# SSD chunks: the state product in three fp32r products of high and low halves

## The chip, the core and the metric

The kernel runs on one core of one Trainium2 chip. The metric is the time of one execution of the whole program on the device, in microseconds (us). Lower is better. All inputs lie in HBM when it starts, and all outputs are in HBM when it ends.

## The reference

The program is one inference step of a small two-layer encoder trunk on two groups of frames that share the weights: 1024 new frames ("prompt") and 32 frames of a running stream ("sample"). Layer one is a Mamba-2 SSD mixer, layer two an HGRN2 mixer; each is followed by a SwiGLU feed-forward part. The change touches only the SSD scan, which works in chunks of frames:

```python
def step(S, inp):
    xc, dtc, Bc, Cc = inp
    cum = jnp.cumsum(dtc * Ag, axis=1)
    ...
    xdt = xc * dtc[..., None]
    cb = jnp.einsum('btgn,bsgn->btsg', Cc, Bc)
    y = jnp.einsum('btsg,btsgh,bsghp->btghp', cb, decay, xdt)
    y = y + jnp.einsum('btgn,bghpn->btghp', Cc, S) * jnp.exp(cum)[..., None]
    last = cum[:, -1]
    w_end = jnp.exp(last[:, None] - cum)
    S = jnp.exp(last)[..., None, None] * S + jnp.einsum('bsgh,bsghp,bsgn->bghpn', w_end, xdt, Bc)
    return S, y
```

The last `einsum` is the state product: over the frames of a chunk, B (128 state entries) times the weighted x (8 heads of 64 entries, 512 in all). It is added to the decayed state S. Everything is float32.

## The kernel before

**Halves and phases.** The 1056 frames are worked in two halves: h = 0 has 512 prompt frames, h = 1 the other 512 and the 32 sample frames. The SSD layer runs first (to about 835 us), then its feed-forward part, then the HGRN2 layer and its own. Activations lie transposed, with features on the partitions and frames along the free axis.

**Large products.** Weights and activations are each split into a high half, rounded to fp32r by a copy on ScalarE, and a low half, the remainder, made by a subtraction on VectorE (`split` and `wsplit`). A product then is three TensorE matmuls per 128 rows, high x high, high x low and low x high, accumulated in PSUM: lines L316, L317 and L318 in `product`. Their outputs are called mm. Most of TensorE's time goes there.

**The SSD chunks.** For each half and each of 4 groups g (8 heads) the kernel walks over chunks of 128 frames: 4 in half 0, 4 and the one of 32 sample frames in half 1. That makes 16 + 20 = 36 calls of `ssd_chunk`, 32 of them with 128 frames and 4 with 32. A chunk takes the score product of B and C (L540), transposes x (L545), forms `xdt` and `xw` on VectorE (two ways of weighting x), builds the decay matrices `dec` on ScalarE (Relu with a bias for each of 8 heads, then Exp) and VectorE, transposes B (L561), copies it to `Btok` on ScalarE, multiplies the old state with C (L568), makes the state product (L571: B as weights 128 x 128, `xw` as the moving 512 columns, both fp32), adds it to S on VectorE, and computes the eight heads' outputs (L582). Each of these eight matmuls has weights of only 64 columns, and even and odd heads go to the lower and upper 64 output partitions. The helper lines L98 (`act`, ScalarE), L101 (`tt`, VectorE) and L104 (`stt`, VectorE) stand for all calls of these helpers, so one goes by tile names there: `fixed<-sc` on ScalarE is the copy to `Btok`, `yh<-Y` and `yl<-Y,yh` are a split elsewhere.

**Order.** A scheduler lays out each engine's instructions ahead of time: from the code's order, from a few priorities and from the times at which it believes operands ready, it picks the next instruction of each engine. Each engine then works its list strictly in order, and waits on semaphores where an operand is late. Between the steps of a chunk, TensorE is given large products (outputs mm) of other work: output projections, gate projections and the convolution inputs of the next group. So what a chunk's instructions follow on TensorE is chosen by the scheduler, and it can put a large product, or another step of the chunk, between any two matmuls.

**PSUM.** Five banks (mm) serve the large products, three (sc) rotate among all small results of the chunks.

Of the kernel before, what the change touches and what calls it, by code (L numbers as in the profile page):

```python
# [8 lines left out]
F32 = mybir.dt.float32  # L9
F32R = mybir.dt.float32r  # L10
U32 = mybir.dt.uint32
AF = mybir.ActivationFunctionType
# [4 lines left out]
P = 128  # L17
# [23 lines left out]

TW = 552
FIXED = 14368
BUFS = {"x": 12, "ys": 8, "cb": 4, "xd": 2, "de": 2, "ec": 2, "ss": 1, "xr": 2, "n": 4, "w": 3}
WIDTH = {k: TW for k in BUFS}


@with_exitstack
def trunk_kernel(ctx, tc, x_prompt, x_sample, state_ssd, cache_conv, state_hgrn,
# [5 lines left out]
    V, A, G, PE = nc.vector, nc.scalar, nc.gpsimd, nc.tensor  # L55

    cp = ctx.enter_context(tc.tile_pool(name="cp", bufs=1))
    tp = ctx.enter_context(tc.tile_pool(name="tp", bufs=1))
# [7 lines left out]
    def nm(s):  # L66
        uid[0] += 1
        return f"{s}_{uid[0]}"

    def T(tag, s, dt=F32):  # L70
        return tp.tile([P, WIDTH[tag]], dt, tag=tag, bufs=BUFS[tag], name=nm(s))

    def slot(tag, s):
        return T(tag, s, F32R) if isinstance(tag, str) else tag

    rings = {"diag": (0, 2), "cbm": (2, 2), "Btok": (4, 2), "hT": (0, 2), "hSp": (2, 4), "fss": (4, 2), "nco": (0, 1)}
    at = {}

    def small(s, w=P):

        at[s] = at.get(s, -1) + 1
        if s == "hec":
            return hec[at[s] % 3][:, :w]
        first, n = rings[s]
        return smalls[first + at[s] % n][:, :w]
# [11 lines left out]
    def act(out, in_, f, **kw):  # L97
        A.activation(out=out, in_=in_, func=f, **kw)  # L98

    def tt(out, a, b, op, eng=None):  # L100
        (eng or V).tensor_tensor(out=out, in0=a, in1=b, op=op)  # L101
# [23 lines left out]
    MUL, ADD, SUB = ALU.mult, ALU.add, ALU.subtract  # L125
# [5 lines left out]
    def place(w):  # L131
        used[0] += -(-w // 16) * 16
        return fixed[:, used[0] - -(-w // 16) * 16:][:, :w]
# [33 lines left out]
    xr = place(9)  # L167
# [362 lines left out]
    @lifted("chunk")  # L530
    def ssd_chunk(h, g, c, S, loads, u):
        o, n, smp = CHUNKS[h][c]
        Bt, Ct, xs, Y = u["x"][0], u["x"][1], u["x"][2:], u["Y"]
        cols, elast = dts[h]
        xo = o + (3 if smp else 0)
        Bx, Cx = Bt[:, xo:xo + n], Ct[:, xo:xo + n]
        h0 = g * 8
        cums, ec = loads
        ps = psum_sc()
        PE.matmul(ps[:n, :n], Bx, Cx, start=True, stop=True)  # L540
        cbm = small("cbm")
        tt(cbm[:n, :n], ps[:n, :n], cmask[:n, :n], MUL)
        ps = psum_sc()
        for j in range(4):
            PE.transpose(ps[:n, j * P:(j + 1) * P], xs[j][:, xo:xo + n], ident)  # L545
        x3 = ps[:n, :].rearrange("p (h q) -> p h q", q=64)
        xdt, xw = T("xd", "xdt")[:, :512], T("xd", "xw")[:, :512]
        tt(xdt[:n, :].rearrange("p (h q) -> p h q", q=64), x3,
           cols[:n, c, h0:h0 + 8].unsqueeze(2).to_broadcast([n, 8, 64]), MUL)
        tt(xw[:n, :].rearrange("p (h q) -> p h q", q=64), x3,  # L550
           cols[:n, c, 64 + h0:64 + h0 + 8].unsqueeze(2).to_broadcast([n, 8, 64]), MUL)
        for q in range(2):
            cb3 = T("de", "dec")[:, :512].rearrange("p (h t) -> p h t", t=P)
            for i in range(4):
                hh = 32 + h0 + 4 * q + i
                act(cb3[:n, i, :n], cums[q][:n, i, :n], AF.Relu, scale=-1.0, bias=cols[:n, c, hh:hh + 1])
            cums[q] = cb3
            act(cb3[:n, :, :n], cb3[:n, :, :n], AF.Exp, scale=-1.0)
            tt(cb3[:n, :, :n], cb3[:n, :, :n], cbm[:n, :n].unsqueeze(1).to_broadcast([n, 4, n]), MUL)
        ps = psum_sc()  # L560
        PE.transpose(ps[:n, :P], Bx, ident)  # L561
        Btok = small("Btok")
        act(Btok[:n, :], ps[:n, :P], AF.Copy)
        if ec is not None:
            y2 = psum_sc()
            y23 = y2.rearrange("p (j t) -> p j t", t=P)
            for j in range(4):
                PE.matmul(y23[:, j, :n], S[:, j * P:(j + 1) * P], Cx, start=True, stop=True)  # L568
            tt(ec[:, :, :n], y23[:, :, :n], ec[:, :, :n], MUL)
        pp = psum_sc()  # L570
        PE.matmul(pp, Btok[:n, :], xw[:n, :], start=True, stop=True)  # L571
        if ec is None:
            V.tensor_copy(S, pp)
        else:
            S3 = S.rearrange("p (h q) -> p h q", q=64)
            tt(S3, S3, elast[:, h0:h0 + 8, c:c + 1].to_broadcast([P, 8, 64]), MUL)
            tt(S, S, pp, ADD)
        y1 = psum_sc()
        y13 = y1.rearrange("p (j t) -> p j t", t=P)
        for i in range(8):  # L580
            r = 64 * (i % 2)
            PE.matmul(y13[r:r + 64, i // 2, :n], xdt[:n, i * 64:(i + 1) * 64], cums[i // 4][:n, i % 4, :n],  # L582
                      start=True, stop=True)
        yo = Y[:, :, o:o + n]
        if ec is None:
            act(yo, y13[:, :, :n], AF.Copy)
        else:
            tt(yo, y13[:, :, :n], ec[:, :, :n], ADD)
# [720 lines left out]
    for s, dst in ((0, conv_p), (1, conv_s)):  # L1309
        ps = psum_sc()  # L1310
# [41 lines left out]
```

## Time and profile before

| | us |
|---|---|
| Median of 3 runs | 2867.1 |
| Fastest and slowest of them | 2866.38, 2867.78 |
| Span of the profiled execution | 2867.3 |
| TensorE busy in it | 2838.4 (99%) |
| VectorE busy | 2131.5 (74%) |
| ScalarE busy | 1560.3 (54%) |
| Matmuls in it | 19704 |

How to read it: the span runs from the first to the last instruction of one profiled execution. An fp32 matmul shows as two records in a trace, an fp32r matmul as one, and so the 36 state products show as 72. The busy time of a matmul record includes its way through the array, in which the next one already streams. What a matmul costs in a stream is therefore read from the chain of waits, which gives each instruction the time from the end of its predecessor to its own end, or from the distance of starts. The columns of a window's row are, in this order, TensorE, its weight loads, VectorE, ScalarE and GpSimd, each with its busy us and number of instructions, then the granted clock (1.00 is full), the busy share of the DMA engines, and GB/s.

### The profile page before, as it was taken

How to read it: one execution, taken by the hardware profiler on the slowest of the kernel's cores; microseconds unless marked ns; L12 is line 12 of the kernel's file. 1: busy time of each engine (PE TensorE's matmuls, PEld its weight loads, DVE VectorE, ACT ScalarE, POOL GpSimd, SP SyncE). 2: the span in 40 equal slices, each digit the busy share in tenths (PEclk: the TensorE clock that was granted, in tenths of full speed). 3: DMA queues.
4: the chain of work that ended last, by engine and by line, in shares of the span. 5: the costliest groups of instructions: out<-in, count | busy, mean ns of one | idle time of the engine just before them, and what ended most of it. 6: DMA issues, size and time to landing. Idle time of an engine off the chain costs nothing.

```text
span 2867.3 us, 48953 instructions
## 1 busy us (share of the span) xinstructions
PE 2838.4 (99%) x19704; PEld 2614.7 (91%) x19704; DVE 2131.5 (74%) x3686; ACT 1560.3 (54%) x2910; POOL 44.1 (2%) x156
## 2 busy tenths in 40 slices
PE   8999999999999999999999999999999999999998
PEld 8778788999979999999999887899988999999998
DVE  7787887787787877797777556655568877787776
ACT  6665654564644644465444656555564644455544
POOL 1000000000100000000000000000000000000000
PEclk9999999999999999999999999999999999999999
DMA  6444334444322332333323222222222432333332
GB/s 185 111 114 110 95 103 109 115 112 106 103 79 89 119 103 89 111 93 99 96 89 108 81 74 66 75 79 74 80 79 83 124 97 89 117 93 111 104 96 69
DMA packets 394518, 281.56 MB, mean 98 GB/s; under 512 B 16289, under 2 KB 382514, under 8 KB 394290
## 3 DMA queue, kind: packets, MB, share of 16 engines
q1 hardware_dynamic: 394290, 278.43, 33.6%
q8 instruction: 154, 2.52, 0.4%
q14 instruction: 74, 0.61, 0.1%
HBM read 270.57 MB, written 7.82 MB: 97 GB/s over the span
## 4 chain that ended last, share of the span: by engine, by line
PE 93%; DVE 4%; ACT 2%; issue 1%; DMA 0%; SPq 0%; POOL 0%; DVEq 0%; ACTq 0%
PE mm L316 19%; PE mm L317 19%; PE mm L318 19%; PE mm L1005 5%; PE mm L1003 5%; PE mm L1004 5%; PE sc L1005 4%; PE sc L1004 4%; PE sc L1003 4%; PE sc L582 1%; PE sc L571 1%; PE sc L333 1%; PE sc L568 1%; DVE ca L104 1%; PE mm L1277 1%
## 5 line engine op out<-in xcount | busy, mean ns | idle before, releaser
L98 ACT ACTIVATE wh<-raw 128x512 fp32r<-128x512 f32 (+1 forms) x687 | 554.8, 816 | 592.8 <-PE mm L317 491.3
L316 PE MATMUL mm<-xn,wh 128*128 128x272 f32 (+2 forms) x1552 | 523.4, 338 | 1.2 <-ACT pre L98 1.2
L318 PE MATMUL mm<-xn,wl 128*128 128x272 f32 (+2 forms) x1552 | 517.1, 333 | 1.4 <-DVE wl L101 1.4
L317 PE MATMUL mm<-xn,wh 128*128 128x272 f32 (+2 forms) x1552 | 517.9, 334 | 0.0
L101 DVE TENSOR_TENSOR wl<-raw,wh 128x1024 fp32r<-128x1024 f32 (+1 forms) x307 | 372.8, 1216 | 73.8 <-ACT wh L98 52.1
L101 DVE TENSOR_TENSOR fixed<-mm,fixed 128x272 f32<-128x272 f32 (+3 forms) x504 | 259.0, 524 | 199.5 <-PE mm L318 193.3
L316 PE MATMUL mm<-fh,wh 128*128 128x272 f32 (+1 forms) x992 | 322.6, 327 | 0.4 <-ACT fh L98 0.3
L317 PE MATMUL mm<-fl,wh 128*128 128x272 f32 (+1 forms) x992 | 322.7, 326 | 0.0
L318 PE MATMUL mm<-fh,wl 128*128 128x272 f32 (+1 forms) x992 | 322.4, 326 | 0.0
L316 PEld LDWEIGHTS mm<-xn,wh 128*128 128x128 f32 x1552 | 291.8, 188 | 30.9 <-issue 3.0
L318 PEld LDWEIGHTS mm<-xn,wl 128*128 128x128 f32 x1552 | 291.8, 188 | 30.3 <-DVE wl L101 1.8
L317 PEld LDWEIGHTS mm<-xn,wh 128*128 128x128 f32 x1552 | 292.1, 188 | 27.0 <-issue 1.0
L101 DVE TENSOR_TENSOR wh<-raw,wh 128x512 fp32r<-128x512 f32 x380 | 255.8, 685 | 36.6 <-ACT wh L98 33.2
L1003 PE MATMUL mm<-th,wh 128*128 128x272 f32 (+1 forms) x912 | 260.7, 286 | 0.0
L1005 PE MATMUL mm<-th,wh 128*128 128x272 f32 (+1 forms) x912 | 259.9, 285 | 0.0
L1004 PE MATMUL mm<-tl,wh 128*128 128x272 f32 (+1 forms) x912 | 259.6, 285 | 0.0
L316 PEld LDWEIGHTS mm<-fh,wh 128*128 128x128 f32 x992 | 186.3, 188 | 17.1 <-ACT fh L98 1.9
L318 PEld LDWEIGHTS mm<-fh,wl 128*128 128x128 f32 x992 | 186.5, 188 | 15.2
L317 PEld LDWEIGHTS mm<-fl,wh 128*128 128x128 f32 x992 | 186.6, 188 | 14.9 <-DVE fl L101 0.2
L1003 PE MATMUL sc<-xn,wh 128*128 128x272 f32 (+1 forms) x608 | 172.9, 284 | 0.5 <-ACT wh L98 0.5
L1003 PEld LDWEIGHTS mm<-th,wh 128*128 128x128 f32 x912 | 171.8, 188 | 1.6 <-ACT s L98 1.1
L1004 PE MATMUL sc<-xn,wh 128*128 128x272 f32 (+1 forms) x608 | 173.3, 285 | 0.0
(266 smaller groups left out, 6696.6 us busy)
## 6 DMA issues: line engine op xcount, KB each, us to landing
raw<-in_ffn_w_gate_dram SPq DMA_DIRECT2D x88, 512.0 KB, 4.0
raw<-in_ffn_w_up_dram SPq DMA_DIRECT2D x88, 512.0 KB, 4.7
raw<-in_ffn_w_down_dram SPq DMA_DIRECT2D x88, 512.0 KB, 3.5
raw<-in_ssd_in_w_dram SPq DMA_DIRECT2D x80, 512.0 KB, 4.1
raw<-in_hgrn_in_w_dram SPq DMA_DIRECT2D x64, 512.0 KB, 4.2
cumB<-cumd SPq DMA_DIRECT2D x64, 256.0 KB, 4.9
raw<-in_ssd_out_w_dram SPq DMA_DIRECT2D x32, 512.0 KB, 3.7
raw<-in_hgrn_out_w_dram SPq DMA_DIRECT2D x16, 512.0 KB, 3.3
```

Of the source, the lines that this page charges most:

```text
L98: A.activation(out=out, in_=in_, func=f, **kw)
L101: (eng or V).tensor_tensor(out=out, in0=a, in1=b, op=op)
L104: V.scalar_tensor_tensor(out=out, in0=a, scalar=s, in1=b, op0=op0, op1=op1)
L316: PE.matmul(ps[:, :bn], a, mh, start=(k == 0), stop=False)
L317: PE.matmul(ps[:, :bn], a, ml, start=False, stop=False)
L318: PE.matmul(ps[:, :bn], b, mh, start=False, stop=(k == n - 1))
L333: PE.matmul(ps[:, :bn], ones, tot[:, b0:b0 + bn], start=True, stop=True)
L568: PE.matmul(y23[:, j, :n], S[:, j * P:(j + 1) * P], Cx, start=True, stop=True)
L571: PE.matmul(pp, Btok[:n, :], xw[:n, :], start=True, stop=True)
L1003: PE.matmul(ps[:, :n], a, mh, start=(k == 0 and not more), stop=False, skip_group_check=True)
L1004: PE.matmul(ps[:, :n], a, ml, start=False, stop=False, skip_group_check=True)
L1005: PE.matmul(ps[:, :n], b, mh, start=False, stop=(k == 3), skip_group_check=True)
```

## The change

`Btok` (in fp32) is gone. The transposed B is copied to `Bh` in fp32r by ScalarE, and VectorE subtracts it from the PSUM result to make `Bl`. The weighted x gets a high half `xwh` (a copy by ScalarE) and a low half `xwl` (a subtraction by VectorE). The state product is Bh x xwh + Bh x xwl + Bl x xwh, three fp32r matmuls into one PSUM accumulation. The halves have new buffers of their own, and nothing else loses one. In the changed kernel the lines further down move: the transpose of B is L564, the state product L576 to L578, the old state's product L573, and the heads' outputs L589.

```diff
-BUFS = {"x": 12, "ys": 8, "cb": 4, "xd": 2, "de": 2, "ec": 2, "ss": 1, "xr": 2, "n": 4, "w": 3}
+BUFS = {"x": 12, "ys": 8, "cb": 4, "xd": 2, "xh": 2, "de": 2, "ec": 2, "ss": 1, "xr": 2, "n": 4, "w": 3}
...
-    rings = {"diag": (0, 2), "cbm": (2, 2), "Btok": (4, 2), "hT": (0, 2), "hSp": (2, 4), "fss": (4, 2), "nco": (0, 1)}
+    rings = {"diag": (0, 2), "cbm": (2, 2), "hT": (0, 2), "hSp": (2, 4), "fss": (4, 2), "nco": (0, 1)}
...
         xdt, xw = T("xd", "xdt")[:, :512], T("xd", "xw")[:, :512]
+        xwh, xwl = T("xh", "xwh", F32R)[:, :512], T("xh", "xwl", F32R)[:, :512]
...
+        act(xwh[:n, :], xw[:n, :], AF.Copy)
+        tt(xwl[:n, :], xw[:n, :], xwh[:n, :].bitcast(F32), SUB)
...
-        Btok = small("Btok")
-        act(Btok[:n, :], ps[:n, :P], AF.Copy)
+        bt = tp.tile([P, 2 * P], F32R, tag="bt", bufs=2, name=nm("bt"))
+        Bh, Bl = bt[:, :P], bt[:, P:]
+        act(Bh[:n, :], ps[:n, :P], AF.Copy)
+        tt(Bl[:n, :], ps[:n, :P], Bh[:n, :].bitcast(F32), SUB)
...
-        PE.matmul(pp, Btok[:n, :], xw[:n, :], start=True, stop=True)
+        PE.matmul(pp, Bh[:n, :], xwh[:n, :], start=True, stop=False)
+        PE.matmul(pp, Bh[:n, :], xwl[:n, :], start=False, stop=False)
+        PE.matmul(pp, Bl[:n, :], xwh[:n, :], start=False, stop=True)
```

The scheduler lays the lists out anew, so the change also moves instructions that the diff does not name. Behind the SSD layer the lists of all engines are the same as before. Three places, all in `ssd_chunk`.

First, TensorE in the second chunk of the first group (the chunk that runs at 97 us in the profile before). Names: `sc` are small results in PSUM, `xw` the weighted x, `dec` the decay matrices of four heads, `fixed` the pool in which `Btok` lies. Before:

```order
L316 MATMUL mm_1230<-xn,wh_1224 128x512
L571 MATMUL sc_1046<-xw_1020,fixed 128x512
L582 MATMUL sc_1050<-dec_1023,xdt_1019 64x128 x4
L582 MATMUL sc_1050<-dec_1030,xdt_1019 64x128 x4
L540 MATMUL sc_1080<-ca_443,ca_288 128x128
```

and now:

```order
L318 MATMUL mm_1262<-xn,wl_1257 128x512
L576 MATMUL sc_1060<-xwh_1029,bt_1051 128x512
L589 MATMUL sc_1066<-dec_1035,xdt_1027 64x128 x3
L577 MATMUL sc_1060<-xwl_1030,bt_1051 128x512
L578 MATMUL sc_1060<-xwh_1029,bt_1051 128x512
L589 MATMUL sc_1066<-dec_1035,xdt_1027 64x128
L316 MATMUL mm_1321<-xn,wh_1315 128x512
L589 MATMUL sc_1066<-dec_1042,xdt_1027 64x128 x4
L317 MATMUL mm_1321<-xn,wh_1315 128x512
```

The eight heads' outputs (64x128 rows), one unbroken run before, now stand in three runs of 3, 1 and 4, with matmuls of another shape between them.

Second, TensorE in the first chunk of 32 sample frames (at 500 us before; there the contraction has only 32 rows, and L507 transposes the state for output). Before:

```order
L318 MATMUL mm_5003<-xn,wl_4997 128x272
L571 MATMUL sc_4913<-xw_4887,fixed 128x512
L582 MATMUL sc_4917<-dec_4890,xdt_4886 64x32 x4
L582 MATMUL sc_4917<-dec_4897,xdt_4886 64x32 x4
L507 MATMUL sc_4927<-fixed 128x128 x4
```

and now:

```order
L316 MATMUL mm_5171<-xn,wh_5164 128x272
L576 MATMUL sc_5079<-xwh_5048,bt_5070 128x512
L589 MATMUL sc_5085<-dec_5054,xdt_5046 64x32 x4
L589 MATMUL sc_5085<-dec_5061,xdt_5046 64x32 x4
L507 MATMUL sc_5095<-fixed 128x128 x3
L577 MATMUL sc_5079<-xwl_5049,bt_5070 128x512
L578 MATMUL sc_5079<-xwh_5048,bt_5070 128x512
L507 MATMUL sc_5095<-fixed 128x128
```

The second and third product, again of 32 rows, now stand between transposes of 128 rows, behind the heads' outputs.

Third, VectorE in the second chunk of half 1, group 0 (at 470 us before). Before:

```order
L101 TENSOR_TENSOR xw_4543<-sc_4537,fixed 128x512
L101 TENSOR_TENSOR dec_4553<-dec_4553,fixed 128x512
L101 TENSOR_TENSOR ec_4414<-sc_4563,ec_4414 128x512
L101 TENSOR_TENSOR fixed<-fixed 128x512
L101 TENSOR_TENSOR wl_4820<-raw_4817,wh_4819 128x1024
```

and now:

```order
L101 TENSOR_TENSOR xw_4679<-sc_4673,fixed 128x512
L101 TENSOR_TENSOR dec_4693<-dec_4693,fixed 128x512
L101 TENSOR_TENSOR bt_4702<-sc_4700,bt_4702 128x128
L101 TENSOR_TENSOR xwl_4681<-xw_4679,xwh_4680 128x512
L101 TENSOR_TENSOR ec_4542<-sc_4705,ec_4542 128x512
L101 TENSOR_TENSOR fixed<-fixed 128x512
```

The two low halves stand behind the second decay matrix and ahead of the old state's share `ec`. On TensorE the same chunk's heads now stand in two runs of 4, with L577 and L578 between them, and 17 instead of 12 large products stand between L573 and L576 (before: L568 and L571).

## The prediction

> **What bounds the kernel now.** I read the page first, then the stage's own window, then who waits for whom there, then the chain of waits around a few state products. From the page, TensorE's busy time and the shares of the chain:
>
> ```profile
> PE 2838.4 (99%) x19704; PEld 2614.7 (91%) x19704; DVE 2131.5 (74%) x3686; ACT 1560.3 (54%) x2910; POOL 44.1 (2%) x156
> ...
> PE 93%; DVE 4%; ACT 2%; issue 1%; DMA 0%; SPq 0%; POOL 0%; DVEq 0%; ACTq 0%
> ```
>
> The same for the 747 us in which the chunks run, and for the densest 24 us of them, the first group (TensorE, weight loads, VectorE, ScalarE):
>
> ```profile
> 88.00:835.00 747.00, 743.23 (x4992) 647.98 (x4992) 602.66 (x953) 425.56 (x876) 36.62 (x133) 1.00 0.40 105
> 88.00:112.00 24.00, 24.00 (x169) 18.17 (x169) 22.39 (x51) 18.55 (x51) 0.49 (x2) 1.00 0.45 118
> ```
>
> And TensorE's idle time in the same 747 us, by whom it waited for:
>
> ```profile
> PE mm L316 <- DVE fixed L101: 1.3, 1, 1.3
> PE mm L318 <- DVE wl L101: 0.9, 1, 0.9
> PE sc L333 <- DVE sq L101: 0.4, 1, 0.4
> ```
>
> TensorE bounds this stage: it is busy 743 of 747 us at full clock, and its longest wait is one of 1.3 us. VectorE has 19% to spare, ScalarE 43%. So the sum is one of TensorE's time in its own stream, plus what new waits add.
>
> **What goes and what comes on TensorE.** The chain around the second chunk (start, us, what), where each row is the time from the end of the one before to its own end:
>
> ```profile
> 96.98 0.23 PE mm L316
> 97.21 0.86 PE sc L571 x2
> 98.07 1.02 PE sc L582 x16
> 99.09 0.42 PE sc L540 x2
> 99.51 0.23 PE mm L317
> ```
>
> The fp32 state product costs 0.86 us, two records of 0.43. An fp32r product of the same 512 columns (L316, L317) costs 0.23, so three cost 0.69 to 0.70. Each of 36 chunks saves 0.16 us: **-5.7 us**. That is the whole gain, and it needs the three to run in a stream.
>
> The Trainium skill (FP8 and Floating Point Precision, section TensorE Precision Notes) says that a true fp32 product takes four passes through the array. Four passes of 0.23 would be 0.92, and the estimate from the page is a saving of 36 x 0.23 = 8.3 us in place of 5.7. The row has 0.86, and the sum goes by it.
>
> They do not run in a stream everywhere. I went through TensorE's list by the shape of the weights. The eight heads' outputs (64 columns) stood in 37 runs, and now stand in 60: 24 breaks in place of 1. Of the 24, 13 fall behind an odd head, as the first order excerpt's 3 | 1, and 11 behind an even one, as its 1 | 4. What a break costs can be read from the one break that exists, in which L333 cuts the eight heads after the third, beside a run that is whole:
>
> ```profile
> 470.40 0.91 PE sc L571 x2
> 471.32 1.02 PE sc L582 x16
> 472.34 0.32 PE mm L316
> 472.66 0.12 PE mm L317
> ...
> 777.12 0.58 PE sc L582 x6
> 777.71 1.05 PE sc L333 x2
> 778.76 0.80 PE sc L582 x10
> ```
>
> First, the product behind the run: L316 costs 0.32 where L317, of the same size, costs 0.12. Leaving the 64-column shape costs 0.20; L333, the same shape as L571, shows it too, at 1.05 in place of 0.86. Second, the run: whole it is 1.02, broken 0.58 + 0.80 = 1.38. With a fixed price e of entering the shape, p for an even and an odd head together, and s for a lone head: e + 4p = 1.02, e + p + s = 0.58, e + 2p + s = 0.80. That gives p = 0.22, e = 0.14, s = 0.22. A lone head costs as much as a pair, since the other half of the columns is empty. So an even break costs e and the exit, 0.34, and an odd one a further s, 0.56 (the 1.38 - 1.02 + 0.19 of the rows). Above the one that is there: 12 x 0.56 + 11 x 0.34 = 6.7 + 3.7 = **+10.4 us**.
>
> The Trainium skill (TensorEngine Tiling (Array Packing), section Tiling Modes, Key Properties) has a rule that speaks against this change: a change of tiling mode drains TensorE, while another tile in the same mode does not. The trace agrees at each of these exits with 0.20 us.
>
> The sample chunks (32 rows) change shape more often too:
>
> ```profile
> 500.22 1.05 PE sc L571 x2
> 501.27 0.58 PE sc L582 x16
> 501.86 0.58 PE sc L507 x4
> ...
> 503.81 0.22 PE sc L507 x2
> ```
>
> L571 costs 1.05 there in place of 0.86, so entering costs 0.19. The first L507 run behind costs 0.58 in place of 4 x 0.11, so leaving costs 0.14, or 0.20 as above. By the list, TensorE enters the 32-row shape 5 times more often than before (once in three of the sample chunks, twice in the fourth): 5 x 0.36 = **+1.8 us**.
>
> **What comes on VectorE and ScalarE.** The nearest rows for the four added kinds, by form:
>
> ```profile
> L101 DVE TENSOR_TENSOR yl<-Y,yh 128x512 fp32r<-128x512 f32 x16 | 10.9, 683 | 0.0
> L101 DVE TENSOR_TENSOR fixed<-sc,fixed 128x128 f32<-128x128 f32 x32 | 9.1, 285 | 42.8 <-PE sc L540 42.8
> L98 ACT ACTIVATE yh<-Y 128x512 fp32r<-128x512 f32 x16 | 9.9, 622 | 0.6 <-DVE Y L104 0.6
> L98 ACT ACTIVATE fixed<-sc 128x128 f32<-128x128 f32 x33 | 8.9, 269 | 7.5 <-PE sc L561 6.1 <-PE sc L194 1.5
> ```
>
> The low halves cost VectorE 0.68 + 0.29 = 0.97 us a chunk, 35 us in all: 603 becomes 638 of 747 us. `xwh` costs ScalarE 0.62 a chunk, 22 us in all: 426 becomes 448. `Bh` replaces the `Btok` copy at 0.27. I cost all of that at nothing, because TensorE's other products cover it. If the cover were gone, 36 x (0.62 + 0.68) = 47 us is what the longer way from `xw` to the last product is worth.
>
> Is it covered? Before, the scheduler put L571 only just behind its operand:
>
> ```profile
> 469.39 0.68 DVE L101 TENSOR_TENSOR xw<-sc,fixed 128x512 f32<-128x512 f32 x1
> 469.99 0.68 DVE L101 TENSOR_TENSOR dec<-dec,fixed 128x512 f32<-128x512 f32 x1
> ...
> 470.24 1.08 PE L571 MATMUL sc<-xw,fixed 128*128 128x512 f32 x2
> ```
>
> `xw` ends at 470.07 and L571 starts 0.17 later. With the new lists (third excerpt): `xwh` can follow on ScalarE from 470.07 to 470.7. VectorE starts a 512-column operation every 0.60, so `bt` starts at 470.6, `xwl` at 470.9, and ends at 471.6. TensorE has five more large products ahead of L576, which brings it to 470.24 + 5 x 0.125 = 470.9, behind `xwh`. L577 comes after that product (0.23), four heads (0.14 + 0.44) and an exit (0.20): 471.9, 0.3 behind `xwl`. So it fits, though with margins of 0.2 to 0.3 us, and there are two such points in a chunk where there was one. Behind L577 stand L578, the rest of the heads and all large products, and VectorE's update of S waits for L578. The rows of L571 show what such a wait has cost so far:
>
> ```profile
> L571 PE MATMUL sc<-xw,fixed x72: 587/592/692, 91.4 to 830.7; 128*128 128x512 f32 x64, 32*128 32x512 f32 x8
> ```
>
> In the chain pieces above it was 0.86 or 0.91, so 0 to 0.05 us. For the one added wait a chunk I take the upper end nearly, 0.04: 36 x 0.04 = **+1.5 us**. The bounds: below, that L571's own 0.05 goes without a successor, 36 x -0.05 = -1.8 us; above, for both waits the 0.10 by which the longest record stands above the median, 72 x 0.10 = 7.2 us.
>
> **Sum:** 2867.3 - 5.7 + 10.4 + 1.8 + 1.5 = 2875.3. The profiled span (2867.3) is 0.2 above the median of the runs (2867.1), so the forecast is **2875 us**, 0.28% slower. A measurement of this kernel tells about 0.2% (5.7 us) from no change. The sum's own range is 2871 (waits at -1.8, and even breaks at the exit's 0.20 alone, 1.5 less) to 2881 (waits at 7.2).
>
> **Rivals.**
>
> *Breaks cost less in the new place (no change).* The waits for `xwl` and the entries and exits may fall into the same time, and the products between the heads are single-record ones, which no row of before shows there. If only the exits are paid, 23 x 0.20 = 4.6 in place of 10.4, the time is 2867.3 - 5.7 + 4.6 + 1.8 = 2868. Against it: L316 behind L582 is a single-record product too, and pays. Chance 0.20.
>
> *Faster.* If three fp32r products hide their shape changes entirely, only the pass saving is left: 2867.3 - 5.7 = 2861.6; with L571's own wait of up to 0.05 gone as well, 2860. This decides where an exit costs under 0.05 us. The 0.20 of the rows above speaks against it. Chance 0.06.
>
> *VectorE becomes the bound in the first group (slower still).* In 88 to 112 us it is busy 22.4 of 24; four chunks' low halves add 3.9, which makes 26.3. If TensorE has not enough other products there, it stands still for 2.3 us, and the tight margins elsewhere fail at 0.10 twice a chunk: 2867.3 - 5.7 + 10.4 + 1.8 + 2.3 + 7.2 = 2883. For it speaks the density; against it that in the list of that group more large products now stand between the steps. Chance 0.16.
>
> *The change doesn't do what it says:* products of the new halves that run at fp32's pace would be 3 x 0.86 a chunk, +62 us in place of -5.7. Every fp32r product of the trace runs at 0.23 for 512 columns, so I leave this under 0.01.
>
> **How the numbers follow.** My forecast has 0.58, the rivals 0.20, 0.06 and 0.16. About 0.10 of the forecast's share lies below 2872.8, the bound of no change. So slower has 0.48 + 0.16 = 0.64, the same 0.10 + 0.20, rounded to 0.30, faster 0.06. The range takes in the no-change rival and reaches to the slow one: 2867 to 2882.
>
> **What would show it.** In the changed profile: 108 records on L576 to L578 at about 0.40 us each, 0.23 apart in the chain where they stand together; a matmul behind a broken run of L589 0.20 longer than its like; L589 in runs of 6 and 10 records that add up to 1.38, or of 8 and 8 that add up to 1.16, in place of 1.02; VectorE near 638 us in the stage; TensorE's waits on `xwh` and `xwl` under 2 us in all. The forecast is wrong if L576 to L578 wait for VectorE by more than 0.1 us each, if exits from L589 into fp32r products cost nothing, or if time moves outside 88 to 840 us, where the lists are the same.

## The result, and the profile after

The changed kernel takes **2885.1 us** (median of 5 runs, 2883.3 to 2885.6); the kernel before, on the same chip, 2867.1 us (2865.8 to 2867.8). The ratio is 1.0061, with a 95% interval of 1.0050 to 1.0072: the change costs 18 us, where 8 were forecast. The direction was right, the size about half of what came, and the time lies outside the range. The profiled execution has a span of 2883.7 us (before: 2867.3).

From the page of the changed kernel, the engines' busy time and the shares of the chain:

```profile
PE 2847.0 (99%) x19740; PEld 2623.8 (91%) x19740; DVE 2159.8 (75%) x3758; ACT 1585.1 (55%) x2946; POOL 55.5 (2%) x156
...
PE 91%; DVE 6%; ACT 2%; issue 1%; DMA 1%; SPq 0%; POOL 0%; DVEq 0%; ACTq 0%
```

TensorE still bounds it, but VectorE's share of the chain went from 4% to 6%, the first sign that TensorE waits for it. The stage of the chunks, now 764 us in place of 747 (us, then TensorE, weight loads, VectorE, ScalarE, GpSimd, then the granted clock):

```profile
88.00:852.00 764.00, 752.86 (x5028) 658.20 (x5027) 630.54 (x1023) 448.12 (x910) 48.02 (x133) 1.00 0.38 103
```

TensorE is busy 10 us more and idle 11 us in place of 4. Whom it waits for in 80 to 860 us (total, times, longest):

```profile
PE mm L318 <- DVE wl L101: 4.6, 4, 1.9
PE mm L316 <- ACT pre L98: 2.2, 2, 1.3
PE mm L316 <- DVE fixed L101: 1.6, 1, 1.6
PE sc L576 <- ACT xwh L98: 0.8, 2, 0.6
PE sc L333 <- DVE sq L101: 0.6, 1, 0.6
PE sc L577 <- DVE xwl L101: 0.6, 1, 0.6
```

The new products wait for `xwh` and `xwl` 1.4 us in all, as forecast. The large products wait 8.4 us, and most of that is for `wl`, the low halves of *weights*, which the change doesn't touch. The chain through the second chunk, where an odd number of heads is cut off (start, us, what):

```profile
98.46 0.23 PE mm L318
98.70 0.23 PE sc L576
98.92 0.58 PE sc L589 x6
99.50 0.43 PE sc L577
99.93 0.23 PE sc L578
100.17 0.36 PE sc L589 x2
100.53 0.42 PE mm L316
100.96 0.59 PE sc L589 x8
101.54 0.43 PE mm L317
```

Three products at 0.23, and every product behind a piece of the heads at 0.42 or 0.43, 0.20 more. The pieces of three, one and four heads cost 0.58, 0.36 and 0.59; the forecast's prices (e = 0.14, p = s = 0.22) make them 0.58, 0.36 and 0.58.

To see the whole, I charged every TensorE record of 88 to 880 us with the time from the end of the one before it to its own end, and summed by what it is:

| us | before | after | difference |
|---|---|---|---|
| state products (with the exits that fall on them) | 32.8 | 34.4 | +1.6 |
| heads | 35.5 | 41.4 | +5.9 |
| large products right behind heads: excess | 6.1 | 5.7 | -0.4 |
| large products elsewhere, excess over 0.25 us (waits) | 4.3 (5 of them) | 11.4 (10) | +7.1 |
| large products elsewhere, smaller excess | 1.1 | 3.2 | +2.1 |
| sum | | | **+16.3** |

TensorE's own stream costs +7.1, against -5.7 + 10.4 + 1.8 + 1.5 = +8.0 in the forecast. The other 9.2 us are large products that wait or run slowly, and the forecast had put them at nothing. (The span grew by 16.4; score products, transposes and the like, which the table leaves out, add little.)

Where the waits stand: 1.18 us each at 516, 623 and 730 us, which are the ends of the first three of the four groups of half 1; 2.15 at 427, the switch to half 1; 1.62 at 145, 1.08 at 753, 1.83 at 806. At a group's end, VectorE in the changed kernel, by time:

```profile
507.36 0.67 DVE L101 TENSOR_TENSOR Ss<-Ss,fixed 128x512 f32<-128x512 f32 x1
...
510.13 0.69 DVE L101 TENSOR_TENSOR Ss<-Ss,sc 128x512 f32<-128x512 f32 x1 [0.83 <-PE sc L578]
...
513.93 0.72 DVE L101 TENSOR_TENSOR sq<-sq,sq 128x544 f32<-128x544 f32 x1
514.56 1.22 DVE L101 TENSOR_TENSOR wl<-raw,wh 128x1024 fp32r<-128x1024 f32 x1
```

and TensorE, which needs that weight half:

```profile
515.84 0.39 PE L318 MATMUL mm<-xn,wl 128*128 128x272 f32 x1 [0.91 <-DVE wl L101]
```

This weight half is the 70th on VectorE's list. Its number identifies it: in every run in which TensorE waits for the 70th, the product that waits is the same one by count of L318. Before, the 70th and the 71st stood here:

```profile
491.37 1.22 DVE L101 TENSOR_TENSOR wl<-raw,wh 128x1024 fp32r<-128x1024 f32 x1
...
500.14 1.20 DVE L101 TENSOR_TENSOR wl<-raw,wh 128x1024 fp32r<-128x1024 f32 x1
501.31 0.69 DVE L101 TENSOR_TENSOR Ss<-Ss,sc 128x512 f32<-128x512 f32 x1
```

Before, the 70th was made at 491.37, in the chunk ahead, long before its first use at 507.08, and the 71st stood between the two updates of S, in a stretch in which VectorE has to wait for TensorE anyway. In the changed list VectorE is a weight half behind: nothing stands between the updates, and the 70th itself comes behind the second update, eight operations on Y and the first `sq`, 0.9 us late. TensorE's last product L578 even delays that second update by 0.83.

### The profile page after: what moved, and what is told of

Read it like the earlier page. It is cut to its first block, busy times and chain, and to the rows that moved or that the text cites. A ratio compares the mean times of both kernels' runs of the same rounds, so it can differ in the third digit from the quotient of the medians.

```text
span 2883.7 us, 49136 instructions
## 1 busy us (share of the span) xinstructions
PE 2847.0 (99%) x19740; PEld 2623.8 (91%) x19740; DVE 2159.8 (75%) x3758; ACT 1585.1 (55%) x2946; POOL 55.5 (2%) x156
## 4 chain that ended last, share of the span: by engine, by line
PE 91%; DVE 6%; ACT 2%; issue 1%; DMA 1%; SPq 0%; POOL 0%; DVEq 0%; ACTq 0%
PE mm L318 18%; PE mm L316 18%; PE mm L317 18%; PE mm L1012 5%; PE mm L1010 5%; PE mm L1011 5%; PE sc L1012 4%; PE sc L1010 4%; PE sc L1011 4%; PE sc L589 1%; PE sc L333 1%; PE sc L573 1%; PE mm L1284 1%; DVE ca L104 1%; DVE fixed L101 1%
## 5 line engine op out<-in xcount | busy, mean ns | idle before, releaser
L318 PE MATMUL mm<-xn,wl 128*128 128x272 f32 (+2 forms) x1552 | 518.8, 335 | 5.1 <-DVE wl L101 5.0
L316 PE MATMUL mm<-xn,wh 128*128 128x272 f32 (+2 forms) x1552 | 521.7, 337 | 1.6 <-ACT pre L98 1.6
L318 PEld LDWEIGHTS mm<-xn,wl 128*128 128x128 f32 x1552 | 292.5, 189 | 36.7 <-DVE wl L101 6.4
L316 PE MATMUL mm<-fh,wh 128*128 128x272 f32 (+1 forms) x992 | 322.7, 327 | 0.5 <-ACT fh L98 0.3
L318 PE MATMUL mm<-fh,wl 128*128 128x272 f32 (+1 forms) x992 | 322.2, 326 | 0.0
L316 PEld LDWEIGHTS mm<-xn,wh 128*128 128x128 f32 x1552 | 292.4, 189 | 29.7 <-ACT pre L98 2.1
L316 PEld LDWEIGHTS mm<-fh,wh 128*128 128x128 f32 x992 | 186.2, 188 | 17.2 <-ACT fh L98 1.9
L318 PEld LDWEIGHTS mm<-fh,wl 128*128 128x128 f32 x992 | 186.5, 188 | 15.2
```

The costliest lines, as they stand in the source:

```text
L316: PE.matmul(ps[:, :bn], a, mh, start=(k == 0), stop=False)
L318: PE.matmul(ps[:, :bn], b, mh, start=False, stop=(k == n - 1))
```

## The experiments

All are edits of the kernel before or of the changed one, run in 5 rounds; the medians are of 4 to 11 times, and the ratios are to runs of the kernel before on the same chips. "Heads' runs" counts the unbroken runs of 64-column products in TensorE's list; the five columns of us are the rows of the table above, each from one profiled execution. Most of these lie within 2 us of the median; that of dve_double is the fastest of its four (2889.2), and the times of no_subs spread from 2867.4 to 2874.0.

| run | median us | ratio, 95% | heads' runs | state product | heads | exits | waits | smaller |
|---|---|---|---|---|---|---|---|---|
| before | 2867.1 | | 37 | 32.8 | 35.5 | 6.1 | 4.3 | 1.1 |
| changed | 2885.1 | 1.0061, 1.0050-1.0072 | 60 | 34.4 | 41.4 | 5.7 | 11.4 | 3.2 |
| no_subs | 2869.0 | 1.0010, 1.0002-1.0019 | 37 | 27.9 | 35.5 | 5.5 | 9.1 | 2.2 |
| before_break | 2882.8 | 1.0052, 1.0038-1.0066 | 73 | 34.2 | 44.6 | 9.5 | 5.9 | 3.2 |
| low_first | 2870.0 | 1.0009, 1.0000-1.0018 | 39 | 28.5 | 36.1 | 5.3 | 9.0 | 2.4 |
| before_dve | 2878.9 | 1.0041, 1.0029-1.0054 | 38 | 33.2 | 36.5 | 5.7 | 14.3 | 3.6 |
| dve_double | 2893.8 | 1.0089, 1.0075-1.0103 | 38 | 33.8 | 37.9 | 6.9 | 18.1 | 3.5 |
| dve_bu | 2876.7 | 1.0032, 1.0020-1.0045 | 37 | 32.8 | 35.5 | 5.7 | 10.1 | 4.1 |
| dve_busb | 2869.3 | 1.0006, 0.9998-1.0015 | 38 | 32.8 | 35.6 | 6.3 | 6.7 | 1.2 |
| dve_xu | 2877.5 | 1.0037, 1.0024-1.0050 | 47 | 33.9 | 37.3 | 8.1 | 5.8 | 1.7 |
| before_swap | 2875.0 | 1.0027, 1.0017-1.0038 | 46 | 35.3 | 36.6 | 8.6 | 4.1 | 2.1 |
| before_bfirst | 2867.0 | 0.9999, 0.9990-1.0008 | 39 | 33.7 | 35.8 | 5.9 | 2.9 | 1.4 |
| no_subs_bfirst | 2867.8 | 1.0002, 0.9993-1.0011 | 38 | 29.4 | 35.6 | 5.7 | 7.4 | 2.1 |
| low_first_bfirst | 2871.4 | 1.0014, 1.0005-1.0023 | 37 | 30.5 | 36.3 | 5.5 | 6.0 | 3.2 |
| low_first_dt | 2873.9 | 1.0023, 1.0014-1.0031 | 37 | 30.4 | 36.4 | 5.5 | 7.1 | 2.7 |
| low_first_wl | 2870.5 | 1.0010, 1.0002-1.0019 | 37 | 30.4 | 36.3 | 5.7 | 6.1 | 3.3 |
| lf_blsb | 2873.5 | 1.0022, 1.0013-1.0032 | 39 | 32.6 | 37.0 | 5.6 | 7.3 | 2.5 |
| low_first_pool | 2908.9 | 1.0144, 1.0130-1.0158 | 38 | 67.7 | 37.1 | 6.0 | 5.9 | 3.6 |
| after_wl50 | 2883.8 | 1.0057, 1.0043-1.0071 | 58 | 33.8 | 40.7 | 5.9 | 12.4 | 3.1 |
| low_first_wl100 | 2871.6 | 1.0016, 1.0008-1.0025 | 39 | 27.3 | 36.0 | 5.5 | 10.3 | 3.9 |

### The passes and the breaks

**no_subs**: the changed kernel without low halves and subtractions, the high product three times.

```diff
-        tt(xwl[:n, :], xw[:n, :], xwh[:n, :].bitcast(F32), SUB)
...
-        tt(Bl[:n, :], ps[:n, :P], Bh[:n, :].bitcast(F32), SUB)
...
-        PE.matmul(pp, Bh[:n, :], xwl[:n, :], start=False, stop=False)
-        PE.matmul(pp, Bl[:n, :], xwh[:n, :], start=False, stop=True)
+        PE.matmul(pp, Bh[:n, :], xwh[:n, :], start=False, stop=False)
+        PE.matmul(pp, Bh[:n, :], xwh[:n, :], start=False, stop=True)
```

> The change without the low halves: both subtractions on VectorE are left out, and all three products take the high halves (the state is only of fp32r precision). ScalarE's copies stay. 37 runs of heads, as before. Theory: only the pass saving is left, 2867 - 5.7 = 2861 to 2863, and TensorE's waits in the stage are as before, about 4 us. Rival A says the same. If the three products do not save 0.16 us a chunk (the change doesn't do what it says): 2867 or more.

Measured 2869.0. The chain around one chunk:

```profile
470.32 0.26 PE sc L574
470.57 0.23 PE sc L575
470.81 0.23 PE sc L576
```

In a stream three products take 0.69 to 0.72, and the state products of the stage fall by 4.9 us: the saving is real. The time does not show it, since at 413 us one wait for a weight half grew from 1.2 to 4.3 us, with a half-clock stretch (last section) at it, though VectorE has nothing added here. That was the first sign that load isn't all of it.

**before_break**: the fp32 kernel, the state product moved between the third and the fourth head, no work added.

```diff
+        for i in range(0, 3):
...
         PE.matmul(pp, Btok[:n, :], xw[:n, :], start=True, stop=True)
+        for i in range(3, 8):
```

> The kernel before, in fp32, with the state product written between the third and the fourth head, and its addition to S behind the heads: no work is added on any engine. The heads stand in 73 runs, with 17 odd breaks and 20 even ones (before 1 and 0). By the prices of the prediction: 16 x 0.56 + 20 x 0.34 = 15.8 us, 2867 + 16 = 2883. If breaks are free (rival A): 2867.

Measured 2882.8, where the prices say 2883. The rival in which breaks cost nothing (2867) falls. The rows bear the prices out: heads +9.1, and the exits, summed over all products right behind heads whatever their line, +7.1, where 8.6 and 7.2 were priced. That the total fits so closely is luck all the same: waits and smaller excess grew too, by 3.7 us, and other rows, above all the state products apart from their exits, fell by about as much. The chain, with the exit on the product behind the heads:

```profile
97.46 0.86 PE sc L577 x2
98.32 0.59 PE sc L580 x8
98.91 0.42 PE sc L540 x2
```

**low_first**: the changed kernel with the product that needs the latest operand, `xwl`, first.

```diff
-        xwh, xwl = T("xh", "xwh", F32R)[:, :512], T("xh", "xwl", F32R)[:, :512]
+        xwh, xwl = [T("xr", s, F32R)[:, :512] for s in ("xwh", "xwl")]
...
-        PE.matmul(pp, Bh[:n, :], xwh[:n, :], start=True, stop=False)
-        PE.matmul(pp, Bh[:n, :], xwl[:n, :], start=False, stop=False)
+        PE.matmul(pp, Bh[:n, :], xwl[:n, :], start=True, stop=False)
+        PE.matmul(pp, Bh[:n, :], xwh[:n, :], start=False, stop=False)
```

> The change with one swap: the product with xwl, the operand that is ready last, is put first of the three, so that the other two can follow at once (the two halves of xw lie in the pool xr, with two more buffers there). All work of the change stays, that of VectorE too. In TensorE's list the heads' outputs now stand in 39 runs (before 37, change 60), 2 odd breaks and 1 even, and the 32-row shape is entered as often as before. Theory (breaks cost about 10 us and 32-row entries 1.8, and about 9 us come from VectorE's added work, which makes weight halves late): 2885 - 9.5 - 1.8 = 2874. Rival A (all of the loss is VectorE's added work, breaks are free): 2885, no better than the change. Rival B (the waits are an accident of the change's lists, not of the added work): 2867 - 5.7 + 0.9 = 2862.

Measured 2870.0: 15 us of the 18 are gone, where the theory had 2874. The edit also gives the two halves of x other buffers (in the pool xr, with two more there). after_wl50 below has these buffers too, with `xwh` first, and takes 2883.8, so the buffers alone do not bring it. With three breaks left in place of 24, state products and heads fall by 11.2 us. The scheduler places a matmul when its operands are ready; with `xwh` first it starts the group early and fills the gap up to `xwl` with heads, with `xwl` first the three come together.

### What the waits at the large products come from

**before_dve** and **dve_double**: the fp32 kernel, plus the change's two VectorE subtractions, read by nothing; once (35 us), and twice.

```diff
+            xu = T("xh", "xu", F32R)[:, :512]
+            tt(xu[:n, :], xw[:n, :], xw[:n, :], SUB)
...
+            bu = tp.tile([P, P], F32R, tag="bu", bufs=2, name=nm("bu"))
+            tt(bu[:n, :], ps[:n, :P], Btok[:n, :], SUB)
```

> The kernel before, in fp32, with the change's VectorE work added and nothing made of it: one subtraction 128x512 of xw from itself and one 128x128 from PSUM a chunk, into buffers that nothing reads. Theory: VectorE's work alone makes weight halves late, 2867 + 7 to 9 = 2874 to 2876, with TensorE's waits in the stage up from 3.6 to about 11 us. Rival A (all of the loss is VectorE's): 2867 + 18 + 5.7 = 2890. Rival B (accident of the lists): 2867 within 3.

> The kernel before with both added VectorE operations done twice a chunk: 70 us in all, VectorE at 672 of the stage's 747 us. 38 runs of heads. If the loss follows VectorE's load: at least twice before_dve's, 2867 + 24 = 2891 or more. If it is an accident of each new list: 2867 to 2880, no more than before_dve.

Measured 2878.9 and 2893.8. In the waits of before_dve and of dve_double:

```profile
PE mm L318 <- DVE wl L101: 5.1, 6, 1.8
PE mm L316 <- ACT pre L98: 3.9, 4, 2.0
```

```profile
PE mm L318 <- DVE wl L101: 9.1, 6, 2.3
```

The excess at each of the three group ends is 0.70 with 35 us added and 2.3 to 2.6 with 70. VectorE's work is not covered, although VectorE stands idle for a sixth of the stage.

**dve_bu, dve_xu, dve_busb**: only the small subtraction (10 us), only the large one (25 us), and the small one from SBUF in place of PSUM; in this order the one line of each is

```diff
+            tt(bu[:n, :], ps[:n, :P], Btok[:n, :], SUB)
...
+            tt(xu[:n, :], xw[:n, :], xw[:n, :], SUB)
...
+            tt(bu[:n, :], Btok[:n, :], Btok[:n, :], SUB)
```

> The kernel before with only the small one of the two added VectorE operations a chunk (128x128 from PSUM, 36 x 0.29 = 10 us in all, where before_dve added 35 and took 11.9 us). 37 runs of heads, as before. If the loss follows VectorE's load: a third or less of before_dve's, 2867 + 3.5 = 2870. If it is an accident of each new list: anywhere from 2865 to 2875, whatever the load.

> The kernel before, and beside it only the 128x512 subtraction of the change (36 x 0.70 = 25 us of VectorE, from SBUF, read by nothing); its list breaks the heads in ten places at an even count, 10 x 0.34 = +3.4 us. If waits follow VectorE's load (0 added at no load, about +10 at 35 us): waits +7, in all 2877 to 2879, with a wait of about 0.5 us at each group's end in half 1. If the bank hold made them: only the breaks, 2870 to 2872. If it is the single list: anything between, and no wait at the groups' ends.

> The kernel before (fp32 product), and beside it the 128x128 subtraction of the change done on VectorE and read by nothing, but from the copy of B in SBUF and not from PSUM; heads in 38 runs with two broken (about +0.9 us). If the PSUM bank held behind VectorE's queue is what makes the waits: 2867 to 2869, long waits at the large products near the 4.3 us of before. If it is VectorE's load or the single list: like the same subtraction from PSUM, 2872 to 2878, long waits 7 to 11 us.

Measured 2876.7, 2877.5 and 2869.3. No load theory fits: 10 us from PSUM cost as much as 25 us, and 10 us from SBUF nothing. dve_xu's 10 us are breaks (heads and exits +3.8), state products (+1.1), a wait of L333 for `sq` (2.7 us) and a half-clock stretch behind it; it has no wait at a group's end. The PSUM bank fits dve_busb's number, so the whole change was tried without the bank being held:

**lf_blsb**: low_first, with the low half of B subtracted from a copy in SBUF.

```diff
+        Btok = small("Btok")
+        act(Btok[:n, :], ps[:n, :P], AF.Copy)
-        tt(Bl[:n, :], ps[:n, :P], Bh[:n, :].bitcast(F32), SUB)
+        tt(Bl[:n, :], Btok[:n, :], Bh[:n, :].bitcast(F32), SUB)
```

> The change with the product of the low half of x first, and the low half of B subtracted from an fp32 copy of B in SBUF (36 more small copies on ScalarE), so that no PSUM bank waits for VectorE; heads in 39 runs, three broken (+1.7 us), state product -4.3 us as measured in the same order. If the bank hold made the waits: 2863 to 2866. If VectorE's load or the list: 2868 to 2872, as the same order did with the subtraction from PSUM.

Measured 2873.5, where the bank's theory said 2863 to 2866 and the others 2868 to 2872. The bank's theory falls; the 36 more copies on ScalarE may be part of the surplus. What dve_bu and dve_busb differ in is the **place of a weight half in VectorE's list**. At the switch to half 1 VectorE runs a scan (L434). Before, a weight half, the 58th, is the first operation behind it:

```profile
412.26 1.27 DVE L434 TENSOR_TENSOR_SCAN dt<-fixed,dt 128x544 f32<-128x544 f32 x1
413.46 1.19 DVE L101 TENSOR_TENSOR wl<-raw,wh 128x1024 fp32r<-128x1024 f32 x1
```

In no_subs the same half is the eighth, four microseconds behind the scan's start, and TensorE stands:

```profile
408.02 1.27 DVE L434 TENSOR_TENSOR_SCAN dt<-fixed,dt 128x544 f32<-128x544 f32 x1
...
412.15 1.22 DVE L101 TENSOR_TENSOR wl<-raw,wh 128x1024 fp32r<-128x1024 f32 x1
```

```profile
413.42 0.59 PE L318 MATMUL mm<-xn,wl 128*128 128x272 f32 x1 [3.81 <-DVE wl L101]
```

In the changed kernel the 58th stands ahead of the scan, and the one that is late is the next, the 59th, with the scan and 13 other operations between them:

```profile
417.33 1.23 DVE L101 TENSOR_TENSOR wl<-raw,wh 128x1024 fp32r<-128x1024 f32 x1
...
419.84 1.27 DVE L434 TENSOR_TENSOR_SCAN dt<-fixed,dt 128x544 f32<-128x544 f32 x1
...
426.17 1.22 DVE L101 TENSOR_TENSOR wl<-raw,wh 128x1024 fp32r<-128x1024 f32 x1
```

Sorted by the place of the 58th, the excess there is (three lists with a priority of 100 bring the halves in another order and are left out):

| place of the 58th half | kernels (VectorE work added) | excess us |
|---|---|---|
| 1st behind the scan | before (0), before_swap (0), before_bfirst (0), dve_busb (10), dve_xu (25), before_dve (35), dve_double (70) | 0.9 to 1.5 |
| 8th behind the scan | no_subs (0), no_subs_bfirst (0), before_break (0), dve_bu (10), low_first_pool (10) | 4.2 to 4.5 |
| 4th ahead of the scan | changed, low_first, low_first_bfirst, after_wl50, lf_blsb (35 each) | 0.3, and 2.2 to 2.8 for the 59th |

The 59th is the 11th operation behind the scan in all of these lists, and TensorE waits for it only in the last row. There VectorE starts it 8.8 us after the 58th (before: 5.6), while TensorE came from the first use of the one to the first use of the other in 6.1 us before. For the 58th the place decides, and the load does not: 0.9 with 70 us added, 4.3 with none. The last row has no list with less work added, so for the changed kernel itself place and load are not told apart here. But where a priority brings both halves ahead (low_first_wl and low_first_wl100 below, with the same work), TensorE waits for neither.

At the group ends both count. In low_first, VectorE has the changed kernel's full load, and the 70th and 71st half stand where they stood before, in the chunk ahead and between the updates of S:

```profile
490.11 1.22 DVE L101 TENSOR_TENSOR wl<-raw,wh 128x1024 fp32r<-128x1024 f32 x1
...
499.31 1.21 DVE L101 TENSOR_TENSOR wl<-raw,wh 128x1024 fp32r<-128x1024 f32 x1
...
501.37 0.69 DVE L101 TENSOR_TENSOR Ss<-Ss,sc 128x512 f32<-128x512 f32 x1 [0.85 <-PE sc L578]
```

It has no wait there. In before_swap (nothing added), dve_bu (10) and dve_xu (25) the half behind the operations on Y is the 71st, which TensorE needs later, and there is no wait either. In the four lists in which the 70th stands there, the excess is 0.70 in before_dve (35), 1.18 in the changed kernel and in after_wl50 (35), and 2.4 in dve_double (70). So the place of the 70th decides whether TensorE waits, and at that place the added work is seen in how long. In the fp32 kernel the 70th falls back there with 35 and 70 us added and not with 10 or 25; low_first shows that 35 us need not push it back.

**before_swap**: the fp32 kernel, `xw` computed ahead of `xdt`, no work added.

```diff
-        tt(xdt[:n, :].rearrange("p (h q) -> p h q", q=64), x3,
-           cols[:n, c, h0:h0 + 8].unsqueeze(2).to_broadcast([n, 8, 64]), MUL)
         tt(xw[:n, :].rearrange("p (h q) -> p h q", q=64), x3,
            cols[:n, c, 64 + h0:64 + h0 + 8].unsqueeze(2).to_broadcast([n, 8, 64]), MUL)
+        tt(xdt[:n, :].rearrange("p (h q) -> p h q", q=64), x3,
+           cols[:n, c, h0:h0 + 8].unsqueeze(2).to_broadcast([n, 8, 64]), MUL)
```

> The kernel before with the two VectorE products that make xdt and xw in the other order, no work added; its list breaks the heads in ten places at an even count, 10 x 0.34 = +3.4 us less the exits that lie beside a wait. By the price of breaks alone: 2870 to 2871, long waits as before (4 us). If a new list alone brings new waits at the large products: 2873 to 2878.

Measured 2875.0, more than the 2870 to 2871 of the breaks alone. Heads and exits are +3.6, as priced (3.4), and the waits as before, but the state products cost 2.5 more:

```profile
471.52 0.12 PE mm L318
471.65 1.08 PE sc L571 x2
```

```profile
470.81 0.68 DVE L101 TENSOR_TENSOR xw<-sc,fixed 128x512 f32<-128x512 f32 x1
```

The first rows are the chain, the last is VectorE. The product takes 1.08 in place of 0.86, and `xw` ends at 471.49, just ahead of it. The view of waits marks nothing there; I read it as a wait too short to be marked, which no run shows directly. 16 more products than before have a first record 0.1 to 0.2 us over its 0.43.

### Attempts to place the operands better

**before_bfirst, no_subs_bfirst, low_first_bfirst**: B's transpose and copy moved ahead of x's, in the kernel before, in no_subs and in low_first.

```diff
+        PE.transpose(ps[:n, :P], Bx, ident)
+        Btok = small("Btok")
+        act(Btok[:n, :], ps[:n, :P], AF.Copy)
+        ps = psum_sc()
...
-        ps = psum_sc()
-        PE.transpose(ps[:n, :P], Bx, ident)
-        Btok = small("Btok")
-        act(Btok[:n, :], ps[:n, :P], AF.Copy)
```

> The kernel before with the transpose of B and its copy written ahead of the transpose of x: the same operations on the same engines, only another list. 39 runs of heads, two even breaks more (+0.7). If the loss follows VectorE's load: 2868. If a new list costs by itself, through waits at the change of halves and in the last group: 2870 to 2875.

> no_subs (no low halves, three products of the high ones) with the transpose of B and its copy written ahead of that of x, the order that cost nothing in the fp32 kernel. 38 runs of heads. If no_subs missed its 2861 because its new list made one long wait at the change of halves (3.8 us and a stretch at half clock behind it): 2867 - 4.9 + 0.3 = 2862 to 2863. If the three products don't pay for another reason: 2869 again.

> low_first with B's transpose, copy and subtraction written ahead of the transpose of x: the whole change, all its work on VectorE, 37 runs of heads, as before. If the waits belong to single lists: 2867 - 4.9 + 1 to 3 = 2863 to 2865, faster than the kernel before. If they follow VectorE's load: 2870, as low_first.

Measured 2867.0, 2867.8 and 2871.4: no change against the versions without it. no_subs_bfirst still has its long wait at 413 us (4.3), so that order did not test what it was made for. In low_first_bfirst a state product of the last group waits 3.2 us for `xwl`, where low_first had a large product wait as long.

**low_first_dt, low_first_wl, after_wl50, low_first_wl100**: a higher priority for the dt operations (100; in low_first_bfirst's order) or for the weight halves (100 in low_first_bfirst's order; 50 in the changed kernel, with the halves of x placed as in low_first; 100 in low_first).

```diff
-    HP = dict(norm=600, gate=100, hgate=0, chunk=0, hchunk=50, hchunkb=0, dt=0, wl=0, hf=0, conv=0)
+    HP = dict(norm=600, gate=100, hgate=0, chunk=0, hchunk=50, hchunkb=0, dt=0, wl=100, hf=0, conv=0)
```

> low_first_bfirst with a scheduler priority for the chain of small operations that computes dt at the change of halves (0 to 100), so that VectorE does it earlier and the weight halves behind it are less late. If the wait at 413 to 430 us comes from there: 1 to 4 us less than low_first_bfirst. If not: the same within 1.5.

> low_first_bfirst with a scheduler priority for the splitting of weights (0 to 100), so that VectorE prefers weight halves to the chunks' operations. If late weight halves are what is left of the loss: 1 to 4 us less than low_first_bfirst. If the chunks' own chain is as tight as the weights': the same or up to 5 us more, with the waits at L576 in place of those at L318.

> The changed kernel with a higher priority for the weight halves (50; and the halves of x in four of the wider buffers, without which it doesn't fit); the list then has them earlier in the first groups and in the last one, at the same place at the ends of the groups of half 1 (3 x 1.18 us) and behind the scan at the half's switch (2.15 us). If a place in VectorE's list makes the waits: those at 145, 752 and 806 us go (up to 4.5 us), the four others stay, 2879 to 2882. If VectorE's load makes them, they only move: 2884 to 2886.

> The order with the low half of x first, with the weight halves' priority at 100; 39 runs of heads, three broken. In the list of the last group they stand earlier, at the half's switch as before (2.15 us). If the place in the list makes the waits: the ones in 737 to 800 us (1.7 + 3.7 us, and the half-clock stretch behind them) shrink, 2864 to 2868. If others take their place: 2869 to 2871, as the same priority did with B's transpose first.

Measured 2873.9, 2870.5, 2883.8 and 2871.6. All four miss a gain. low_first_dt has a new wait of L333 for `sq` (3.4 us). With a priority of 100 the waits for weight halves shrink to 0 and 0.9 us, and as much comes back as waits of L316 for accumulators that ScalarE or VectorE has not read yet (low_first_wl100):

```profile
PE mm L316 <- ACT pre L98: 3.9, 3, 2.0
PE mm L316 <- DVE fixed L101: 3.2, 1, 3.2
PE mm L318 <- DVE wl L101: 0.9, 1, 0.9
```

In after_wl50 the waits at 145, 754 and 807 us stay (1.62, 1.88, 1.99): they are of this second kind and not for weight halves, so my reading of these three places was wrong.

**low_first_pool**: low_first, with `xwl` subtracted on GpSimd.

```diff
-        tt(xwl[:n, :], xw[:n, :], xwh[:n, :].bitcast(F32), SUB)
+        tt(xwl[:n, :], xw[:n, :], xwh[:n, :].bitcast(F32), SUB, G)
```

> low_first with the large subtraction (128x512) on GpSimd, which is 2% busy, in place of VectorE. 38 runs of heads. If the loss follows VectorE's load: 2870 less two thirds of what is left of it there (about 6 us of waits), 2864 to 2866, so below the kernel before. If an accident of the lists: 2867 to 2873. If GpSimd is slow enough that L576 waits for it (it has 12 to 17 large products, 1.5 to 2 us, of cover): 36 us and more on top.

Measured 2908.9. GpSimd takes twice VectorE's 0.68 us (rows by form, then the waits), and nearly every chunk waits for it (35 waits in 36 chunks):

```profile
L101 POOL TENSOR_TENSOR xwl<-xw,xwh 128x512 fp32r<-128x512 f32 x32 | 46.4, 1450 | 378.7 <-ACT xwh L98 363.2 <-DVE xn L101 15.5
```

```profile
PE sc L576 <- POOL xwl L101: 31.2, 35, 3.6
```

No version here is faster than the kernel before.

## Why the prediction was right in direction and short in size

- **The passes, -5.7: right.** no_subs has -4.9 and low_first -4.3 for state products that stand in a stream.
- **The breaks, +10.4: right.** Heads +5.9, where 12 x 0.36 + 11 x 0.14 = 5.9 was in that sum. The exits, summed over all products right behind heads whatever their line, are +4.5 where 23 x 0.20 = 4.6 was in it; nearly all of that falls on the state products. In before_break the same prices hold. The rival with cheap breaks falls.
- **The 32-row entries, +1.8: about right.** In the trace nine state products of 32 rows behind another shape take 0.42 or 0.43 in place of 0.23 (before, four enter), so five more entries are +1.0; the L507 products cost 0.5 more than before. What other exits from 32 rows add lies in the smaller excess.
- **Waits of the state products, +1.5: right in sum** (1.4), wrong in form: not 0.04 in each chunk, but three waits of 0.2 to 0.6 us, all in the last group (809 to 820 us). That the sum fits is luck.
- **VectorE near 638 us in the stage:** it is 630.5. The added operations start 0.60 and 0.20 us after the ones ahead of them and overlap by the rest, so 36 x 0.80 = 29 us is what they add to busy time (measured 28).
- **"I cost all of that at nothing, because TensorE's other products cover it": this step failed.** It measured +9.2 us (7.1 of waits, 2.1 of smaller excess). The check behind it followed only the way from `xw` to L577, and the price given for a lost cover (47 us) was for that way too. What was not covered is the work *queued behind* on VectorE, above all the low halves of the weights. In numbers: 3 x 1.18 = 3.5 us at the group ends, which the experiments tie to the place of one weight half at each end (the 70th, and later the 84th and 98th) and to the work ahead of it; 0.6 us at the switch to half 1 (0.3 and 2.15 for the 58th and 59th, where before 1.16 and a wait of 0.70 for an accumulator stood), tied to places in the list; 1.7 us for the half-clock stretch that follows it (below); some 3 us net at 145, 753 and 806 to 823 us, where L316 waits for accumulators; and 0.4 us spread over many products. What moves the waits for accumulators from list to list stays open.
- **The rival nearest in time, VectorE as the bound of the first group (2883), was wrong in place:** there is no long wait in 88 to 112 us, and VectorE is busy 20.7 of these 24 us. The first group's chunks lose 1.2 us on broken heads and nothing on state products.
- **"Time moves outside 88-840 us":** it doesn't; the lag is 16.2 us at 827 us and 16.4 at the end.

The clue was there before the run. The third order excerpt has a row `wl` as the last of VectorE's list before, and none in the rows of the change: weight halves had moved back. I read the excerpt for `xwl` alone.

## What to carry to other kernels

When a change adds work to an engine that feeds the bounding one, don't ask only whether the new operands come in time: go through that engine's in-order list and see which operations for *other* consumers now stand further back, and which waits they stood in. Where products accumulate and their operands arrive at different times, write the one with the latest operand first, so that the group goes in one piece; here that edit was worth 15 of 18 us, 11 of them in state products and heads. And on TensorE count the changes of tile shape (0.20 us to leave 64-column products, 0.14 to enter them), not only the passes.

## What was not expected of the hardware

**A short wait can halve TensorE's clock.** Behind the wait at 427 us in the changed kernel, the pitch of the products goes from 0.125 to 0.23 us after one more microsecond, and stays there for 3.4 us:

```profile
427.44 0.39 PE L318 MATMUL mm<-xn,wl 128*128 128x272 f32 x1 [1.88 <-DVE wl L101]
...
428.31 0.29 PE L318 MATMUL mm<-xn,wl 128*128 128x272 f32 x1
428.43 0.38 PE L316 MATMUL mm<-xn,wh 128*128 128x272 f32 x1
428.60 0.43 PE L317 MATMUL mm<-xn,wh 128*128 128x272 f32 x1
428.83 0.43 PE L318 MATMUL mm<-xn,wl 128*128 128x272 f32 x1
```

The windows there have the granted clock at 0.50 (the column ahead of the last two):

```profile
428.50:431.90 3.40, 3.40 (x17) 3.40 (x16) 3.40 (x5) 3.36 (x11) 2.51 (x3) 0.50 0.98 309
```

Every such stretch in these runs, the idle end of the program aside, is 3.41 us long, or two of them, 6.83, and one costs 1.7 us, half its length at a clock of 0.50. All gaps of over 3.2 us in the stage ended in one or were followed by one (no_subs 3.8, dve_bu 3.9, before_break 3.7), and, over all runs, 13 of the 21 gaps between 1.8 and 3.2 us: 1.88 in the changed kernel and 1.96 in low_first_wl100, but not 1.88 in low_first nor 2.44 in dve_bu. The Trainium skill (TensorE: Matmul & The Clock Gate, section What's actually happening) states a free-running window of 3413 ns, with the half clock after an idle one of about 3.4 us; its section Why this matters for your kernels warns of gaps over about 3 us. The length agrees with these traces; that a gap of 1.9 us can be enough does not follow from it, and the measurement decides.

One more: near 1784 us, outside the stage and in code that none of the kernels changes, such a stretch is there in some of the profiles (in both that are compared above) and missing in others. The wait of 1.04 us ahead of it is the same in before, which has the stretch, and in no_subs, which has not. So single spans differ by 1.7 us without a cause in the kernels that I know of, and a stretch can follow a gap of 1 us as well.
